# An encoder in fp32 from three products: one more seven-product pair in each first half of down, and two kept differences made in place

## The chip, the cores and the metric

The kernel runs on one core of a Trainium2 chip. The metric is the device time of one execution in microseconds. The names of the engines are those of the profile: PE (TensorE, the matmuls), DVE (VectorE), ACT (ScalarE), POOL (GpSimd) and SP (SyncE, which here only issues transfers).

## The reference

Two encoder layers over 256 tokens of width 2048 in float32. Each has an attention (differential attention in layer 0, windowed grouped-query attention with a sink in layer 1), a cross-attention of four heads into 256 memory tokens, an output projection, and an MLP of width 8192:

```python
for i in range(DEPTH):
    h = rms_norm(x, norm_attn[i])
    mn = rms_norm(mem, norm_mem[i])
    mkv = (mn @ w_mem_kv[i]).reshape(B, MEM_LEN, 2, N_MEM_HEADS, MEM_HEAD_DIM)
    ...
    heads = jnp.concatenate([o.reshape(B, S, MIX_WIDTH), o_m.reshape(B, S, MEM_WIDTH)], axis=-1)
    x = x + heads @ w_out[i]
    h = rms_norm(x, norm_mlp[i])
    x = x + jnp.square(jax.nn.relu(h @ w_up[i])) @ w_down[i]
```

The change touches the last line's second product ("down"), and a little of the key normalisation in layer 1 and of `mn @ w_mem_kv`.

## The kernel before

**The arithmetic.** A float32 value is split into a high part (a cast on ACT, L450) and a low part (the rest, a subtraction on DVE, L451). A product is three matmuls: high by high, low by high, high by low (L542, L543 and L544 in the projections with pairs; L503 to L505 in the others). The two splits of every weight piece of 128x1024 are the main work of ACT and DVE.

**Pairs.** Two pieces of weights and the hidden features that go with them form a 2x2 product of blocks. A plain pair does it with eight products, 24 matmuls of 128x512. A "fast" pair, in `seven`, does it with seven, 21 matmuls; for that it needs sums of weight pieces (`a` and `b`, L364 and L365 on DVE, each then split) and differences of hidden features. Part of the sums is made ahead in DRAM by POOL's transfers (`make_sums`, L299 a copy and L303 an accumulating add; the buffers are called `madesum`).

**Stages.** Each layer goes through the input projection with attention, the output projection, up (eight chunks), and down. Down has two halves of the output (half 0 and half 1), each of 32 pairs j. In the profiled execution layer 0's half 0 is 763 to 927 us and its half 1 927 to 1089; layer 1's are 1738 to 1902 and 1902 to 2062. The tuple `LATE` names the 19 fast pairs of half 1, and `FAST` those of half 0: they follow a pattern of two fast pairs and one plain.

**Differences that are kept.** Half 0 and half 1 need the same differences of hidden features. `keep` makes them (`differences`: L553, L555, L556 and a split) while up still runs, and ACT's queue stores them to DRAM (L1071, `kept<-h`); POOL's queue reads them back two pairs ahead of their use (`load_kept`, L1186, `h<-kept`). A small scheduler runs such steps: `tick` is called between pairs, and a `Task` waits for a number of ticks. For the last chunks of up the waits are in `KEEP_LAST`, so that the differences of j=28 and j=29 are made after the start of down.

**Hidden features that are away.** The features of chunks 6 to 14 go to DRAM too (`hid`), and SP brings them back (L375, `t2k<-hid`) into a ring of eight buffers `t2k`. SP's queue is in order: a load that waits for its buffer holds up all behind it. So are the loads of weights (`raw`, L395; `blk` and `big`, L343) and of `madesum` (L346) on the same queue. An engine's instructions also run in the order written; the order of the program is fixed when it is built.

**Keys and memory.** In layer 1 the keys are normalised by `norm_T`, whose steps wait `ROWS_GAP` between them and end with the transposes of L664 on PE. The memory tokens are loaded by `load_mem` and split by `make_x2` in a part of their own (`mem_part`).

Of the kernel before, what the change touches and what calls it, by code (L numbers as in the profile page):

```python
# [15 lines left out]
F32R = mybir.dt.float32r  # L16
# [6 lines left out]
P = 128  # L23
# [15 lines left out]
WAIT = 2  # L39
# [11 lines left out]
AHEAD = 2  # L51
WARM = 10
LATE = (2, 4, 5, 7, 8, 10, 11, 13, 14, 16, 17, 19, 20, 22, 23, 25, 26, 28, 29)
FAST = tuple(j for j in LATE if j not in (11, 20))
AWAY = range(6, 15)
LATE_BLK = LATE[2::2]
LOOK = 3
MORE = 3
KEEP_AFTER = (2, 6, 10, 14)
KEEP_LAST = (10, 18, 26, 34)  # L60
KEEP_GAP = 2
SUM_AT = {0: 44, 1: 2}
SUM_GAP = ({"in": 4, "mem": 4, "out": 4, "up": 9}, {"in": 4, "mem": 8, "out": 10, "up": 7})
# [11 lines left out]
def trunk(ctx: ExitStack, tc: tile.TileContext, xin, xtok, memin, memtok, posrel, gcol, rows,  # L75
# [104 lines left out]
    def Light(f, gap):  # L180
        return Stage(f, gap, gap, True)
# [271 lines left out]
    def make_x2(X2, k, src, g):  # L453
        t = X2.new(k)
        split_gain(t[:, 0, :], t[:, 1, :], src, g)
# [175 lines left out]
                nc.vector.tensor_tensor(u[n][t], own[n][t], u[n][t], op=ALU.add)  # L631
        return u

    def norm_T(ps, st, nseg, g, later=False):

        dim = 512 // nseg
        qn = []
        hi = blk([P, 4, S], F32R)
        lo = blk([P, 4, S], F32R)

        ms = small(2 * nseg)

        def squares():
            for t in range(2):
                sq = t2k([P, 512])
                nc.scalar.activation(sq, ps[t], AF.Square)
                m = ms[:, t * nseg:(t + 1) * nseg]
                nc.vector.tensor_reduce(m, sq.rearrange("p (n d) -> p n d", d=dim), axis=AX.X, op=ALU.add)
                nc.vector.tensor_scalar(m, m, 1.0 / dim, st[:, t:t + 1], op0=ALU.mult, op1=ALU.add)

        def rows():
            rs = small(2 * nseg)
            inv_sqrt(rs, ms, 2 * nseg)
            for t in range(2):
                q = t2k([P, 512])
                nc.vector.tensor_tensor(q.rearrange("p (n d) -> p n d", d=dim), ps[t].rearrange("p (n d) -> p n d", d=dim),
                                        rs[:, t * nseg:(t + 1) * nseg].unsqueeze(2).broadcast_to([P, nseg, dim]), op=ALU.mult)
                qn.append(q)

        def tr():  # L660
            for t in range(2):
                pt = bank()
                for h in range(4):
                    nc.tensor.transpose(out=pt[:, h * P:(h + 1) * P], in_=qn[t][:, h * P:(h + 1) * P], identity=ident)  # L664
                ts = slice(t * P, (t + 1) * P)
                split_gain(hi[:, :, ts], lo[:, :, ts], pt.rearrange("p (h s) -> p h s", s=P), g)

        if not later:
            squares()
        return (hi, lo), Task([Light(squares, 1), Light(rows, ROWS_GAP), tr][not later:], wait=WAIT if later else 1, gap=WAIT)  # L670

    def val_f32(v, ps, st):
        for t in range(2):
# [293 lines left out]
    def load_mem(i):  # L967
        mem_raw[i] = quad("h2", (P, 4, S), F32)
        nc.sync.dma_start(mem_raw[i], memin[:, 1024 * i:1024 * i + 1024].rearrange("p (k s) -> p k s", s=S))

    def mem_ahead(j):
        if j == 5:
            load_mem(0)

    def mem_part(layer, qm, qd, H2):
        M2 = Halves()

        def before(j):
            if j % 2 == 0:
                if j:  # L980
                    mem_raw.pop(j // 2 - 1)
                if j < 6:
                    load_mem(j // 2 + 1)
            for k in (2 * j, 2 * j + 1):
                src = mem_raw[j // 2][:, k % 4, :]
                make_x2(M2, k, src, gc[:, G_MEM + layer * KT + k:G_MEM + layer * KT + k + 1])

        ps = chunk_tok(f"mem{layer}", 0, M2, before)
        kT, kd = norm_T(ps, mst, 4, gc[:, G_MK + layer:G_MK + layer + 1], layer == 0)
        vbox = [None, None]  # L990
        heads = [plain_head(h, h, qm, kT, vbox, None, None, H2, 12 + h) for h in range(4)]
        firsts = [Task(h[:2], (qd, kd)) for h in heads]
        ps = chunk_tok(f"mem{layer}", 1, M2)
        flush([kd])
        vbox[0], vbox[1] = val_split(ps, mst)
        for i, h in enumerate(heads):
            done_heads[12 + i] = Task(h[2:], [firsts[i]])
# [54 lines left out]
    def mlp(layer, X2, last):  # L1052
# [7 lines left out]
        def hidden(j):  # L1060
            return hT[j // 2].rearrange("p k s -> p (k s)")[:, (j % 2) * 512:(j % 2) * 512 + 512]

        def keep(j, wait):

            def make():
                box.append(quad("h2", (P, 2, 512)))
                differences(box[0], hidden(j))

            def store():
                kept[j] = dp.tile([P, 2, 512], F32R, name=nm("kept"))  # L1070
                nc.scalar.dma_start(as32(kept[j]), as32(box.pop()))  # L1071

            box = []
            Task([Light(make, KEEP_GAP), Light(store, 0)], wait=wait)

        def h2_of(j):
            t2 = quad("h2", (P, 2, 512))
# [11 lines left out]
        def to_hidden(q, n, u, i, tag):  # L1089
            c = 2 * q + n  # L1090
            if i == 0:
                hT.append(wide[:, 5] if c == 15 else blk([P, 4, S], F32))
            pt = bank(tag)
            for oo in range(2):
                for t in range(2):
                    o = 2 * i + oo
                    nc.tensor.transpose(out=pt[:, oo * S + t * P:oo * S + (t + 1) * P], in_=u[n][t][:, o * P:(o + 1) * P], identity=ident)  # L1097
            j = 2 * c + i
            nc.scalar.activation(hidden(j), pt, AF.Relu)
            nc.scalar.activation(hidden(j), hidden(j), AF.Square)  # L1100
            if c in AWAY:
                hidden_in[j] = dp.tile([P, 512], F32, name=nm("hid"))
                nc.gpsimd.dma_start(hidden_in[j], hidden(j))
            if any(j in fast_pairs(f"down{layer}", h) for h in range(2)):
                keep(j, KEEP_AFTER[2 * n + i] if q < 7 else KEEP_LAST[2 * n + i])

        for q in range(8):
            tag, other = ("mm", "aux") if q % 2 == 0 else ("aux", "mm")
# [43 lines left out]
        for half_ in range(2):  # L1152
# [28 lines left out]
            diff_in = {}  # L1181

            def load_kept(j):
                if j in fast:
                    diff_in[j] = quad("h2", (P, 2, 512))
                    nc.gpsimd.dma_start(diff_in[j], kept[j])  # L1186

            load_kept(1)
            for j in range(32):
# [4 lines left out]
                    ats.append(h2_of((j + 1) % 32))  # L1194
                load_kept(j + 2)
                two.append(piece(f"down{layer}", half_, 2 * j + 1))
                at = ats.popleft()
                if last and half_ == 1 and j >= 30:
                    held.append((j, two, at))
# [62 lines left out]
    for g in range(3):  # L1262
# [20 lines left out]
        kT, kd = norm_T(ps, st0, 8, gc[:, G_AK:G_AK + 1])  # L1283
        for h in range(4):
            done_heads[4 * g + h] = Task(diff_head(h, qT, kT, v, bias, H2, 4 * g + h), [qd, kd] + rows_done)
    ps = chunk_tok("a", 9, X2, mem_ahead)
    qm, qd = norm_T(ps, st0, 4, gs[:, 2:3])
    mem_part(0, qm, qd, H2)
    X2 = out_proj(0, H2)
# [6 lines left out]
    make_sums(1)  # L1296
    kv = key_values(X2)
    row_stats(st1)
    kT, kd = norm_T(kv[0], st1, 4, gc[:, G_BK:G_BK + 1])
    vv = val_split(kv[1], st1)  # L1300
    for g in range(3):
        ps = chunk_tok("b", g, X2)
        qT, qd = norm_T(ps, st1, 4, gs[:, 1:2])
        for h in range(4):
            n = 4 * g + h
            done_heads[n] = Task(plain_head(h, n // 3, qT, kT, vv, bias, sink[:, n:n + 1], H2, n), [qd, kd])
    ps = chunk_tok("b", 3, X2, mem_ahead)
    qm, qd = norm_T(ps, st1, 4, gs[:, 3:4])
    mem_part(1, qm, qd, H2)
    X2 = out_proj(1, H2)  # L1310
# [71 lines left out]
```

## Time and profile before

| what | us |
|---|---|
| median of 3 runs | 2066.44 (2066.3 to 2066.57) |
| the profiled execution | 2068.06 |
| its span, first to last instruction | 2066.3 |
| PE busy | 2059.5 (100%) |
| DVE busy | 1824.9 (88%) |
| ACT busy | 1295.9 (63%) |
| POOL busy | 190.5 (9%) |

PE's busy time counts matmuls that overlap, and so a busy share of 100% doesn't say that each takes as long as its row shows. The profile's list of waits says for what an engine stood idle; the windows give each engine's busy time in a stretch; the timeline has single instructions with their start, length, and the idle time before them. The granted clock of PE was 1.000 throughout.

### The profile page before, as it was taken

How to read it: one execution, taken by the hardware profiler on the slowest of the kernel's cores; microseconds unless marked ns; L12 is line 12 of the kernel's file. 1: busy time of each engine (PE TensorE's matmuls, PEld its weight loads, DVE VectorE, ACT ScalarE, POOL GpSimd, SP SyncE). 2: the span in 40 equal slices, each digit the busy share in tenths (PEclk: the TensorE clock that was granted, in tenths of full speed). 3: DMA queues.
4: the chain of work that ended last, by engine and by line, in shares of the span. 5: the costliest groups of instructions: out<-in, count | busy, mean ns of one | idle time of the engine just before them, and what ended most of it. 6: DMA issues, size and time to landing. Idle time of an engine off the chain costs nothing.

```text
span 2066.3 us, 28900 instructions
## 1 busy us (share of the span) xinstructions
PE 2059.5 (100%) x9966; PEld 1711.5 (83%) x9966; DVE 1824.9 (88%) x2659; ACT 1295.9 (63%) x1933; POOL 190.5 (9%) x292
## 2 busy tenths in 40 slices
PE   9999999999999999999999999999999999999999
PEld 7888888888888888888888888888888888888887
DVE  7677787898998999999999778889999999999998
ACT  7467665556566576767756556556566566676764
POOL 1200111100011100000002110000001111000000
PEclk9999999999999999999999999999999999999999
DMA  9678997877898998989978887577799999898994
GB/s 318 242 240 269 279 290 227 276 232 245 277 292 285 308 322 300 389 282 322 365 295 274 262 251 262 174 234 244 246 296 298 311 306 349 309 379 308 329 374 144
DMA packets 176099, 589.08 MB, mean 285 GB/s; under 512 B 20464, under 2 KB 21488, under 8 KB 174576
## 3 DMA queue, kind: packets, MB, share of 16 engines
q1 hardware_dynamic: 134128, 439.36, 59.5%
q0 software_dynamic: 36208, 127.94, 23.7%
q10 hardware_dynamic: 5616, 19.93, 2.4%
q8 instruction: 78, 1.28, 0.2%
q14 instruction: 69, 0.57, 0.1%
HBM read 552.42 MB, written 108.13 MB: 320 GB/s over the span
## 4 chain that ended last, share of the span: by engine, by line
PE 94%; DVE 3%; DMA 2%; issue 1%; ACT 1%; SPq 0%; DVEq 0%; ACTq 0%
PE mm L543 12%; PE mm L544 12%; PE mm L542 12%; PE aux L544 11%; PE aux L542 11%; PE aux L543 11%; PE mm L503 6%; PE mm L504 6%; PE mm L505 6%; DVE lo L451 1%; PE aux L687 1%; PE mm L1097 1%; PE aux L664 1%; PE aux L1097 1%; DMA kept<-h 1%
## 5 line engine op out<-in xcount | busy, mean ns | idle before, releaser
L451 DVE TENSOR_TENSOR lo<-raw,hi 128x1024 fp32r<-128x1024 f32 (+1 forms) x492 | 583.5, 1205 | 116.6 <-ACT hi L450 115.7
L450 ACT CAST hi<-raw 128x1024 fp32r<-128x1024 f32 (+1 forms) x492 | 495.6, 1035 | 287.8 <-PE mm L505 95.7
L503 PE MATMUL mm<-hi,x 128*128 128x512 f32 x576 | 231.5, 404 | 0.1
L504 PE MATMUL mm<-lo,x 128*128 128x512 f32 x576 | 225.6, 392 | 0.2 <-DVE lo L451 0.2
L505 PE MATMUL mm<-hi,x 128*128 128x512 f32 x576 | 225.2, 391 | 0.0
L450 ACT CAST h<-big 128x1024 fp32r<-128x1024 f32 (+1 forms) x100 | 100.4, 1021 | 131.7 <-DVE big L291 84.3
L542 PE MATMUL mm<-hi,x 128*128 128x512 f32 x464 | 181.3, 391 | 0.0
L543 PE MATMUL mm<-lo,x 128*128 128x512 f32 x464 | 180.7, 389 | 0.0
L544 PE MATMUL mm<-hi,x 128*128 128x512 f32 x464 | 180.6, 389 | 0.0
L543 PE MATMUL mm<-lo,h 128*128 128x512 f32 (+1 forms) x448 | 174.2, 389 | 1.3 <-DVE lo L451 1.3
L542 PE MATMUL mm<-hi,h 128*128 128x512 f32 (+1 forms) x448 | 174.1, 389 | 0.0
L544 PE MATMUL mm<-hi,h 128*128 128x512 f32 (+1 forms) x448 | 173.7, 388 | 0.0
L450 ACT CAST hi<-big 128x1024 fp32r<-128x1024 f32 (+1 forms) x138 | 120.8, 902 | 77.1 <-PE aux L544 35.9
L542 PE MATMUL aux<-hi,x 128*128 128x512 f32 x400 | 156.3, 391 | 0.0
L544 PE MATMUL aux<-hi,x 128*128 128x512 f32 x400 | 155.7, 389 | 0.0
L543 PE MATMUL aux<-lo,x 128*128 128x512 f32 x400 | 155.7, 389 | 0.0
L542 PE MATMUL aux<-hi,h 128*128 128x512 f32 x392 | 152.8, 390 | 0.0
L544 PE MATMUL aux<-hi,h 128*128 128x512 f32 x392 | 152.5, 389 | 0.0
L543 PE MATMUL aux<-lo,h 128*128 128x512 f32 x392 | 152.5, 389 | 0.0
L451 DVE TENSOR_TENSOR lo<-big,hi 128x1024 fp32r<-128x1024 f32 (+1 forms) x138 | 139.6, 1032 | 6.8 <-ACT hi L450 6.4
L451 DVE TENSOR_TENSOR h<-big,h 128x1024 fp32r<-128x1024 f32 (+1 forms) x100 | 116.8, 1179 | 30.8 <-ACT h L450 30.0
L505 PEld LDWEIGHTS mm<-hi,x 128*128 128x128 f32 x576 | 108.1, 188 | 23.8 <-DVE x L447 0.2
(318 smaller groups left out, 4452.5 us busy)
## 6 DMA issues: line engine op xcount, KB each, us to landing
raw<-in_w_up SPq DMA_DIRECT2D x164, 512.0 KB, 6.5
madesum<-in_w_down POOLq DMA_DIRECT2D x140, 512.0 KB, 6.6
raw<-in_w_down SPq DMA_DIRECT2D x112, 512.0 KB, 6.5
big<-in_w_up SPq DMA_DIRECT2D x92, 512.0 KB, 5.0
raw<-in_w_a SPq DMA_DIRECT2D x72, 512.0 KB, 5.3
h<-kept POOLq DMA_DIRECT2D x72, 512.0 KB, 6.9
raw<-in_w_out SPq DMA_DIRECT2D x52, 512.0 KB, 5.3
big<-in_w_down SPq DMA_DIRECT2D x46, 512.0 KB, 5.7
```

What stands on the lines that cost most here:

```text
L450: nc.scalar.copy(hi, src)
L451: return nc.vector.tensor_tensor(lo, src, as32(hi), op=ALU.subtract)
L503: nc.tensor.matmul(ps[t], lhsT=xh, rhs=hi[:, ws], start=(k == 0), stop=False)
L504: nc.tensor.matmul(ps[t], lhsT=xh, rhs=lo[:, ws], start=False, stop=False)
L505: nc.tensor.matmul(ps[t], lhsT=xl, rhs=hi[:, ws], start=False, stop=(k == KT - 1))
L542: nc.tensor.matmul(acc_, lhsT=x(0), rhs=w2[0][:, ws], start=first_, stop=False)
L543: nc.tensor.matmul(acc_, lhsT=x(0), rhs=w2[1][:, ws], start=False, stop=False)
L544: nc.tensor.matmul(acc_, lhsT=x(1), rhs=w2[0][:, ws], start=False, stop=last_)
L664: nc.tensor.transpose(out=pt[:, h * P:(h + 1) * P], in_=qn[t][:, h * P:(h + 1) * P], identity=ident)
L687: nc.tensor.transpose(out=pt[:, kt * S + qt * P:kt * S + (qt + 1) * P], in_=p_of(qt)[:, kt * P:(kt + 1) * P], identity=ident)
L1097: nc.tensor.transpose(out=pt[:, oo * S + t * P:oo * S + (t + 1) * P], in_=u[n][t][:, o * P:(o + 1) * P], identity=ident)
```

## The change

1. `FAST` leaves out only pair 26 of `LATE`, where it left out 11 and 20: half 0 of down has 18 fast pairs instead of 17 in each layer, and the kernel 74 instead of 72 in all. Pair 26 becomes plain in half 0, and 11 and 20 become fast.
2. The differences for j=28 and 29 are no longer made at the start of down. In half 0 `make_kept` makes them two pairs ahead of their use, from the hidden features that SP brought back, and uses them from where they are; then they are stored for half 1. Half 0 doesn't read them back.
3. The key normalisation of layer 1 asks for a gap of two steps instead of one ahead of its transposes.
4. The memory tokens are loaded one step sooner, and split one step sooner.

```diff
--- before.py
+++ after.py
-FAST = tuple(j for j in LATE if j not in (11, 20))
+FAST = tuple(j for j in LATE if j != 26)
...
-KEEP_LAST = (10, 18, 26, 34)
+KEEP_LATE = (28, 29)
...
-    def norm_T(ps, st, nseg, g, later=False):
+    def norm_T(ps, st, nseg, g, later=False, rows_gap=ROWS_GAP):
...
-        return (hi, lo), Task([Light(squares, 1), Light(rows, ROWS_GAP), tr][not later:], wait=WAIT if later else 1, gap=WAIT)
+        return (hi, lo), Task([Light(squares, 1), Light(rows, rows_gap), tr][not later:], wait=WAIT if later else 1, gap=WAIT)
...
-    def mem_ahead(j):
-        if j == 5:
-            load_mem(0)
+    mem_x2 = {}
+
+    def memory(layer, j):
+        if j == 0:
+            mem_x2[layer] = Halves()
+        if j % 2 == 0:
+            if j:
+                mem_raw.pop(j // 2 - 1)
+            if j < 6:
+                load_mem(j // 2 + 1)
+        for k in (2 * j, 2 * j + 1):
+            src = mem_raw[j // 2][:, k % 4, :]
+            make_x2(mem_x2[layer], k, src, gc[:, G_MEM + layer * KT + k:G_MEM + layer * KT + k + 1])
+
+    def mem_ahead(layer):
+
+        def ahead(j):
+            if j == 4:
+                load_mem(0)
+            if j == 7:
+                memory(layer, 0)
+
+        return ahead
...
         def before(j):
...
+            if j < 7:
+                memory(layer, j + 1)
...
+        def store_kept(j, t2):
+            kept[j] = dp.tile([P, 2, 512], F32R, name=nm("kept"))
+            nc.scalar.dma_start(as32(kept[j]), as32(t2))
...
-            Task([Light(make, KEEP_GAP), Light(store, 0)], wait=wait)
+            Task([Light(make, KEEP_GAP), Light(lambda: store_kept(j, box.pop()), 0)], wait=wait)
...
             if any(j in fast_pairs(f"down{layer}", h) for h in range(2)):
-                keep(j, KEEP_AFTER[2 * n + i] if q < 7 else KEEP_LAST[2 * n + i])
+                if j not in KEEP_LATE:
+                    keep(j, KEEP_AFTER[2 * n + i])
...
             def load_kept(j):
-                if j in fast:
+                if j in fast and (half_ or j not in KEEP_LATE):
                     diff_in[j] = quad("h2", (P, 2, 512))
                     nc.gpsimd.dma_start(diff_in[j], kept[j])
+
+            def make_kept(j):
+                if half_ == 0 and j in KEEP_LATE:
+                    diff_in[j] = quad("h2", (P, 2, 512))
+                    differences(diff_in[j], hids[j])
+                    Task([Light(lambda t2=diff_in[j]: store_kept(j, t2), 0)], wait=KEEP_GAP)
...
                 two.append(piece(f"down{layer}", half_, 2 * j + 1))
+                make_kept(j + 2)
...
-    ps = chunk_tok("a", 9, X2, mem_ahead)
+    ps = chunk_tok("a", 9, X2, mem_ahead(0))
...
-    kT, kd = norm_T(kv[0], st1, 4, gc[:, G_BK:G_BK + 1])
+    kT, kd = norm_T(kv[0], st1, 4, gc[:, G_BK:G_BK + 1], rows_gap=2)
...
-    ps = chunk_tok("b", 3, X2, mem_ahead)
+    ps = chunk_tok("b", 3, X2, mem_ahead(1))
```

**DVE, start of down's half 0 in layer 0.** The first four rows are pair 10's; then stands the second of the two kept differences, j=29, and behind it the pieces of pair 11. `lo`, `x` and `h` are low parts of weights, of sums and of hidden features; `blk1672` holds the hidden features of j=29. Before:

```order
L451 TENSOR_TENSOR lo1762_8271<-blk1657_7819,hi1761_8270 128x1024 [waits Activation_49]
L451 TENSOR_TENSOR h21768_8288<-blk1240_5908,h21768_8288 128x512 [waits DMASW3_49]
L451 TENSOR_TENSOR x21767_8281<-blk1656_7818,x21766_8280 128x1024 [waits Activation_49]
L451 TENSOR_TENSOR lo1770_8292<-t2k1734_8141,hi1769_8291 128x512 [waits PE_49]
L553 TENSOR_TENSOR t2k1772_8320<-blk1672_7870 128x256
L555 TENSOR_TENSOR t2k1772_8320<-blk1672_7870,t2k1772_8320 128x128 [waits DVE_49]
L556 TENSOR_TENSOR t2k1772_8320<-blk1672_7870,t2k1772_8320 128x128 [waits DVE_49]
L451 TENSOR_TENSOR h21771_8319<-t2k1772_8320,h21771_8319 128x512 [waits Activation_49]
L451 TENSOR_TENSOR lo1775_8328<-raw1773_8326,hi1774_8327 128x1024 [waits DMAHW2_49,Activation_49]
L451 TENSOR_TENSOR h21778_8338<-blk1240_5908,h21778_8338 128x512 [waits DMASW4_49,DMASW2_49,Activation_49]
```

After, from the same row of pair 10:

```order
L451 TENSOR_TENSOR lo1761_8269<-blk1658_7821,hi1760_8268 128x1024 [waits Activation_49]
L451 TENSOR_TENSOR h21767_8286<-blk1240_5908,h21767_8286 128x512 [waits DMASW5_49]
L451 TENSOR_TENSOR x21766_8279<-big980_4688,x21765_8278 128x1024 [waits Activation_49]
L451 TENSOR_TENSOR lo1770_8292<-t2k1733_8137,hi1769_8291 128x512 [waits PE_49]
L364 TENSOR_TENSOR big980_4688<-big980_4688 128x512 [waits DMAHW5_49,DMAHW1_49]
L451 TENSOR_TENSOR x21776_8330<-big980_4688,x21775_8329 128x1024 [waits PE_49,Activation_49]
L365 TENSOR_TENSOR big980_4688<-big980_4688,t2k1744_8188 128x512 [waits DVE_49]
L451 TENSOR_TENSOR h21779_8339<-blk1240_5908,h21779_8339 128x512 [waits DMASW6_49,PE_49]
```

The three rows of the differences, L553, L555 and L556, and the split behind them are gone from this place, and those of j=28, some 25 rows ahead, are gone as well; the sums of pair 11, a fast one now, follow.

**DVE, the end of half 0 in layer 0, after the change.** The first row is the split of the second sum of pair 25 (`x21925`); `t2k1941` holds the hidden features of j=28, `t2k1951` those of j=29, `lo1931` is the low part of the first piece of pair 26:

```order
L451 TENSOR_TENSOR x21925_8980<-big980_4688,x21924_8979 128x1024 [waits Activation_49]
L451 TENSOR_TENSOR lo1928_8991<-t2k1889_8834,hi1927_8990 128x512 [waits PE_49]
L451 TENSOR_TENSOR h21934_9030<-t2k1921_8973,h21934_9030 128x512 [waits DMAHW4_49]
L451 TENSOR_TENSOR h21942_9068<-t2k1933_9026,h21942_9068 128x512 [waits DMAHW7_49,DMASW0_49,Activation_49]
L553 TENSOR_TENSOR t2k1947_9078<-t2k1941_9064 128x256 [waits DMAHW0_49]
L555 TENSOR_TENSOR t2k1947_9078<-t2k1941_9064,t2k1947_9078 128x128 [waits DVE_49]
L556 TENSOR_TENSOR t2k1947_9078<-t2k1941_9064,t2k1947_9078 128x128 [waits DVE_49]
L451 TENSOR_TENSOR h21946_9077<-t2k1947_9078,h21946_9077 128x512 [waits Activation_49]
L553 TENSOR_TENSOR t2k1960_9134<-t2k1951_9112 128x256 [waits DMAHW6_49]
L555 TENSOR_TENSOR t2k1960_9134<-t2k1951_9112,t2k1960_9134 128x128 [waits DVE_49]
L556 TENSOR_TENSOR t2k1960_9134<-t2k1951_9112,t2k1960_9134 128x128 [waits DVE_49]
L451 TENSOR_TENSOR lo1931_9020<-raw1929_9018,hi1930_9019 128x1024 [waits Activation_49]
```

Two sets of differences now stand here, and the second waits for a transfer.

**SP, the same place.** Before, with the hidden features of j=28 and 29 in `t2k1942` and `t2k1950`:

```order
L375 DMA t2k1942_9073<-hid1674_7878 128x512 [waits DMAHW3_49,DMASW0_49,DVE_49]
L395 DMA raw1968_9200<-in_w_down 128x1024 [waits DMAHW4_49,DVE_49]
L395 DMA raw1972_9209<-in_w_down 128x1024 [waits DMAHW5_49,DVE_49]
L375 DMA t2k1950_9111<-hid1676_7887 128x512 [waits DMAHW6_49,DMASW1_49,DVE_49]
L346 DMA big980_4688<-madesum840_4055 128x1024 [waits DMAHW7_49,DVE_49]
L343 DMA big980_4688<-in_w_down 128x1024 [waits DMAHW0_49,DVE_49]
L346 DMA big980_4688<-madesum865_4161 128x1024 [waits DMAHW1_49,DVE_49]
```

After, with those of j=28 and 29 in `t2k1941` and `t2k1951`:

```order
L375 DMA t2k1941_9064<-hid1675_7881 128x512 [waits DMAHW0_49,DMASW2_49,DVE_49]
L343 DMA big980_4688<-in_w_down 128x1024 [waits DMAHW1_49,DVE_49]
L395 DMA raw1938_9060<-in_w_down 128x1024 [waits DMAHW2_49,DVE_49]
L395 DMA raw1943_9071<-in_w_down 128x1024 [waits DMAHW3_49,DVE_49]
L343 DMA blk1659_7822<-in_w_down 128x1024 [waits DMAHW4_49,DVE_49]
L346 DMA big980_4688<-madesum886_4256 128x1024 [waits DMAHW5_49,DVE_49]
L375 DMA t2k1951_9112<-hid1677_7890 128x512 [waits DMAHW6_49,DMASW3_49]
L395 DMA raw1971_9208<-in_w_down 128x1024 [waits DMAHW0_49,DVE_49]
```

The load for j=29 stood ahead of the sum loads (`madesum840`, `madesum865`), and now stands behind three loads more, the last of them `madesum886`.

**PE, the key transposes of layer 1.** Before:

```order
L503 MATMUL mm2440_11300<-hi2451_11333,x22019_9428 128x512 [waits Activation_49]
L504 MATMUL mm2440_11300<-lo2452_11334,x22019_9428 128x512 [waits DVE_49]
L664 MATMUL aux2454_11353<-ident_76,t2k2448_11328 128x128 [waits DVE_49]
L664 MATMUL aux2454_11353<-ident_76,t2k2448_11328 128x128 x3
L505 MATMUL mm2440_11300<-hi2451_11333,x22019_9428 128x512
L664 MATMUL aux2455_11360<-ident_76,t2k2449_11330 128x128 [waits DVE_49]
L664 MATMUL aux2455_11360<-ident_76,t2k2449_11330 128x128 x3
L503 MATMUL mm2441_11301<-hi2451_11333,x22019_9428 128x512
```

After:

```order
L503 MATMUL mm2443_11308<-hi2454_11341,x22022_9436 128x512 [waits Activation_49]
L504 MATMUL mm2443_11308<-lo2455_11342,x22022_9436 128x512 [waits DVE_49]
L664 MATMUL aux2460_11379<-ident_76,t2k2451_11336 128x128 [waits DVE_49]
L664 MATMUL aux2460_11379<-ident_76,t2k2451_11336 128x128 x3
L505 MATMUL mm2443_11308<-hi2454_11341,x22022_9436 128x512
L664 MATMUL aux2461_11386<-ident_76,t2k2452_11338 128x128 [waits DVE_49]
L664 MATMUL aux2461_11386<-ident_76,t2k2452_11338 128x128 x3
L503 MATMUL mm2444_11309<-hi2454_11341,x22022_9436 128x512
```

The rows stand in the same order.

More of the change, by code (lines that the diff above doesn't have):

```diff
@@ L969, in load_mem @@
         nc.sync.dma_start(mem_raw[i], memin[:, 1024 * i:1024 * i + 1024].rearrange("p (k s) -> p k s", s=S))
-    def mem_ahead(j):
-        if j == 5:
-            load_mem(0)
+    mem_x2 = {}
[17 more added lines that the diff above has]
+        return ahead
     def mem_part(layer, qm, qd, H2):
-        M2 = Halves()
+        M2 = mem_x2[layer]
         def before(j):
[L979 to L986, printed above, removed]
+            if j < 7:
+                memory(layer, j + 1)
         ps = chunk_tok(f"mem{layer}", 0, M2, before)
@@ L1067, in make @@
                 differences(box[0], hidden(j))
-            def store():
-                kept[j] = dp.tile([P, 2, 512], F32R, name=nm("kept"))
-                nc.scalar.dma_start(as32(kept[j]), as32(box.pop()))
             box = []
-            Task([Light(make, KEEP_GAP), Light(store, 0)], wait=wait)
+            Task([Light(make, KEEP_GAP), Light(lambda: store_kept(j, box.pop()), 0)], wait=wait)
         def h2_of(j):
```

## The prediction

> **What bounds the kernel now.** I read the page's busy times first, then TensorE's waits, then the windows of the four halves of down, and last the timeline around each wait.
>
> ```profile
> span 2066.3 us, 28900 instructions
> PE 2059.5 (100%) x9966; PEld 1711.5 (83%) x9966; DVE 1824.9 (88%) x2659; ACT 1295.9 (63%) x1933; POOL 190.5 (9%) x292
> ...
> PE 94%; DVE 3%; DMA 2%; issue 1%; ACT 1%; SPq 0%; DVEq 0%; ACTq 0%
> ```
> ```profile
> PE mm L543 <- DVE lo L451: 1.3, 2, 0.8
> PE aux L142 <- DVE ones L139: 1.1, 1, 1.1
> PE aux L664 <- DVE t2k L656: 0.7, 1, 0.7
> PE mm L504 <- DVE lo L451: 0.2, 1, 0.2
> PE aux L687 <- DVE t2k L805: 0.2, 1, 0.2
> ```
> TensorE works from end to end, and its named waits sum to 3.5 us of 2066.3. So an edit can win only in two ways: by taking matmuls away, or by taking these waits away. It can lose as much as it likes, if it puts a new wait on TensorE.
>
> ```profile
> 763.20:927.20 164.00, 163.18 (x728) 134.73 (x727) 155.03 (x186) 111.18 (x142) 9.57 (x18) 1.00 0.92 329
> 927.20:1088.60 161.40, 161.40 (x722) 133.94 (x721) 155.54 (x186) 111.67 (x146) 13.08 (x21) 1.00 0.92 329
> 1738.20:1902.00 163.80, 163.30 (x729) 134.81 (x728) 155.97 (x188) 111.57 (x141) 9.57 (x19) 1.00 0.93 337
> 1902.00:2062.00 160.00, 160.00 (x716) 132.84 (x715) 153.05 (x180) 103.99 (x128) 9.48 (x18) 1.00 0.81 291
> ```
> These are down's halves 0 and 1 of both layers (window, length, then busy time of PE, PEld, DVE, ACT, POOL, the granted clock 1.00, the DMA share). VectorE is the runner-up: in layer 0's half 0 it idles 164.00 − 155.03 = 8.97 us. Half 1 does 19 fast pairs with 155.54 busy of 161.40, and TensorE doesn't wait there at all (161.40 of 161.40).
>
> **1. One more fast pair in each first half: −1.36 us.** A plain pair issues 24 matmuls of 128x512 and a fast one 21, so two layers lose 6. A matmul's own duration is no price, since they overlap; the spacing is:
>
> ```profile
> 1054.28 0.39 PE L543 MATMUL aux<-lo,h 128*128 128x512 f32 x1
> 1054.50 0.39 PE L544 MATMUL aux<-hi,h 128*128 128x512 f32 x1
> 1054.73 0.39 PE L542 MATMUL mm<-hi,h 128*128 128x512 f32 x1
> 1054.96 0.39 PE L543 MATMUL mm<-lo,h 128*128 128x512 f32 x1
> ...
> 1059.49 0.39 PE L542 MATMUL mm<-hi,h 128*128 128x512 f32 x1
> ```
> From 1054.73 to 1059.49 one fast pair passes: 4.76 us for 21, or 0.227 each. Six make 1.36; by the duration of 0.39 they would make 2.3. The Trainium skill's "TensorE: Matmul & The Clock Gate", section "Back-to-back issue gap", gives a sustained spacing of about 131 ns at N=512, and about 216 ns for an isolated one; by the first, six matmuls would be an estimated 0.79 us and the sum 0.57 us less. This trace, with its granted clock of 1.00, shows 227 ns, and I take the trace.
>
> The pair costs VectorE more. Its rows in 850 to 920 are:
>
> ```profile
> L451 DVE TENSOR_TENSOR x<-big,x 128x1024 fp32r<-128x1024 f32 x10 | 12.1, 1214 | 0.0
> L451 DVE TENSOR_TENSOR h<-t2k,h 128x512 fp32r<-128x512 f32 x11 | 7.3, 679 | 0.0
> ```
> ```profile
> 1049.87 1.22 DVE L451 TENSOR_TENSOR x<-big,x 128x1024 fp32r<-128x1024 f32 x1
> 1051.01 0.68 DVE L451 TENSOR_TENSOR lo<-t2k,hi 128x512 fp32r<-128x512 f32 x1
> 1051.61 0.68 DVE L364 TENSOR_TENSOR big<-big 128x512 f32<-128x512 f32 x1
> ```
> Start to start these are 1.14 and 0.60. A plain pair is two splits of 1024 and one hidden split of 512, 2.88; a fast one three of 1024 and four of 512 (two sums, half a piece, the hidden), 5.82. So VectorE gets 2.94 more in each half 0: 155.03 + 2.94 = 157.97 busy in about 162 us. Half 1 shows that 155.54 in 161.40 runs without a wait; 4 us of room against its 5.9 is less, but room it is. I cost it at nothing; its cover is the lead that VectorE has over TensorE, and if that is gone, each missing us is one of TensorE. The GpSimd queue's extra copy and add fall at the end of up, ahead of its first loads there; the additional load of half a megabyte of sums and the kept loads dropped nearly cancel in a half that moves 164 x 329 = 54 MB.
>
> **2. The last two kept differences leave the start of down: −1.86 us.** The waits at TensorE's L543 stand there:
>
> ```profile
> 792.84 0.33 ACTq L1071 DMA_DIRECT2D kept<-h  x1
> ...
> 799.02 0.62 ACT L450 CAST h<-blk 128x512 fp32r<-128x512 f32 x1 [2.79 <-DMA kept<-h]
> ...
> 800.63 1.22 DVE L451 TENSOR_TENSOR x<-big,x 128x1024 fp32r<-128x1024 f32 x1 [1.41 <-ACT x L450]
> ...
> 804.78 0.39 PE L542 MATMUL mm<-hi,h 128*128 128x512 f32 x1
> ...
> 805.99 0.50 PE L543 MATMUL mm<-lo,h 128*128 128x512 f32 x1 [0.82 <-DVE lo L451]
> ```
> ```profile
> 1779.48 0.39 PE L542 MATMUL mm<-hi,h 128*128 128x512 f32 x1
> 1780.37 0.50 PE L543 MATMUL mm<-lo,h 128*128 128x512 f32 x1 [0.50 <-DVE lo L451]
> ```
> The store of a kept difference holds its buffer for 6 us, ScalarE's next hidden cast waits 2.79 for that buffer, VectorE then 1.41 for ScalarE's sum, and TensorE in the end 0.82. Start to start TensorE loses 1.21 − 0.23 = 0.98, and 0.11 more since the released matmul takes 0.50 and not 0.39, together 1.09; in layer 1, 0.66 and 0.11, 0.77. The changed order has neither the store nor the differences there, and VectorE is spared this in the same thin stretch:
>
> ```profile
> 814.54 0.41 DVE L553 TENSOR_TENSOR t2k<-blk 128x256 f32<-128x256 f32 x1
> 814.99 0.29 DVE L555 TENSOR_TENSOR t2k<-blk,t2k 128x128 f32<-128x128 f32 x1
> 815.31 0.29 DVE L556 TENSOR_TENSOR t2k<-blk,t2k 128x128 f32<-128x128 f32 x1
> 816.29 0.69 DVE L451 TENSOR_TENSOR h<-t2k,h 128x512 fp32r<-128x512 f32 x1 [0.69 <-ACT h L450]
> ```
> That is 2.4 us with its wait, twice. It pays for the 2.94 of the fast pair at j=11 before that comes. Bounds: both waits go whole (−1.86), or none goes (0) if another buffer is as late. I take −1.86: the store is the only late step of the chain, and it is 2.79 late against 1.1 lost.
>
> **3. The same differences at j=26 and 27: +1.2 us, and the unknown of this sum.** VectorE now makes the difference for j=29 in line, from hidden features that come from DRAM. In the changed order that load stands on SP behind the second sum load of pair 25, whose buffer VectorE frees with the split `x<-big` of pair 25's second sum. Between that split and the L553 that waits for the load VectorE has seven rows, four splits of 512 and the other difference's three, 3.4 us of work. Before, the same load went out 20 us ahead of its use:
>
> ```profile
> 884.81 0.33 SPq L375 DMA_DIRECT2D t2k<-hid  x1
> ```
> ```profile
> 904.92 0.68 DVE L451 TENSOR_TENSOR h<-t2k,h 128x512 fp32r<-128x512 f32 x1
> ```
>
> The half 1 rows above give the positions in the pattern that half 0 now has at j=25. The split of the second sum ends at 1051.09, 3.64 ahead of pair 25's first matmul (1054.73) and 8.40 ahead of pair 26's (1059.49). The sum load goes out ahead of the hidden one, 0.33 on the queue, so the hidden load issues 8.0 ahead of pair 26. With a landing time L, three difference rows (1.0) and the first split of pair 26 (1.2), that split is ready at L − 5.8 past the start of pair 26, where its second matmul needs it at 0.2. TensorE's new wait is about L − 5.8 where that is positive. Landings of this load, by window (855 to 890, 830 to 860, 985 to 1052):
>
> ```profile
> DMA to landing us min/median/max: 4.2/6.2/8.9
> ...
> DMA to landing us min/median/max: 5.8/6.6/8.7
> ...
> DMA to landing us min/median/max: 4.5/5.6/6.2
> ```
> So 0 at 4.2, 0.4 at 6.2, 0.8 at 6.6, 3.1 at 8.9, in each layer. I take 0.6, between the medians of the two windows of half 0, which have the same DMA share: +1.2. The range is 0 to +6.2. What VectorE loses here it has back in the two plain pairs 26 and 27, which cost it 2.88 each of 5.45. The store on ScalarE's queue stands behind the difference, and hidden casts behind the store; they are a pair ahead of their use, so 0.
>
> **4. Key transposes and memory splits: 0.** The wait at L664 is this one:
>
> ```profile
> 1142.61 0.39 PE L504 MATMUL mm<-lo,x 128*128 128x512 f32 x1
> 1143.67 0.66 PE L664 MATMUL aux<-ident,t2k 128*128 128x128 f32 x4 [0.68 <-DVE t2k L656]
> ```
> It costs 1.06 − 0.22 = 0.84. The diff asks for a gap of 2 instead of 1, but in the order both kernels issue the transposes behind the very same matmuls, and VectorE's rows ahead of them are the same. So 0, with −0.84 as the other end. The memory splits do move in layer 1, but TensorE has no wait in the memory projection; 0, at best the 0.2 of L687.
>
> **The sum.** −1.36 − 1.86 + 1.2 + 0 = −2.0 us. The profiled execution took 2068.06 with its span of 2066.3; it stands 1.62 over the median of the runs, and the difference is carried to the median: 2066.44 − 2.0 = 2064.4.
>
> **The rivals.**
> - *The hidden load lands under its cover.* The 4.2 in the window 855 to 890 and all of 985 to 1052 but its upper end speak for it; the medians of half 0 against it. Then −3.2: 2063.2. The Trainium skill's "DMA: Bandwidth & Descriptors", section "Anatomy of one DMA — SWDGE (gpsimd) path", fits 2.0 us plus bytes/436e3; an estimate by it for these 256 KB is 2.6 us, and it would make this rival certain. That fit is for another queue than SP's, and no landing of this load in the windows above is under 4.2, so it adds little to the chance.
> - *The hidden load lands late and the first half turns into a loss.* It is slower than before when the two new waits exceed 3.2, so from L = 7.4 in each layer. At 8.9 the sum is −3.2 + 6.2, or 2069.4. To pass 0.2% the wait would have to be 3.7 in each layer, a landing of 9.5, which none of these windows shows.
> - *The key transposes do get their rows in time*, through other timing ahead of them: −0.84, and with the first rival 2062.4. The unchanged order speaks against it.
> - *Moving the differences doesn't remove the start's wait*, because another late buffer or a late load takes its place: 2064.4 + 1.86 = 2066.3. VectorE's idle of 1.41 having one releaser speaks against it.
>
> **How the numbers follow.** Forecast 0.45; load under cover 0.25; transposes too 0.08; the start's wait stays 0.10; late load 0.12, of which beyond 0.2% less than half. A change of 0.2%, 4.1 us, is what a measurement of this kernel can tell from none; only the third rival with some more gain comes near 2062.3, and only the worst of the second passes 2070.6: faster 0.07, same 0.88, slower 0.05. The range of 8 in 10 goes from 2062.6 (the first rival less 0.6) to 2068.0 (new waits of 2.4 in each layer).
>
> **What would show it.** TensorE's waits on L543 near 806 and 1780 are gone; the count of matmuls is 6 lower; VectorE's L553 stands near 890 with idle time ahead of it put down to `t2k<-hid`, and TensorE waits for a `lo<-raw` just behind (right if it is under 1.5, wrong if it is absent or over 3); L664 keeps its 0.7. The prediction fails if TensorE shows waits for VectorE through the first 60 us of half 0, or anywhere outside these places.

## The result, and the profile after

The changed kernel takes 2064.28 us (median of 22 runs, 2063.13 to 2065.58), the kernel before 2067.76 (22 runs, 2066.07 to 2071.83): a ratio of 0.9983 with an interval of 0.9977 to 0.9989, or 3.5 us less (2.3 to 4.8). The range held the time. The three runs of before that the prediction started from, 2066.3 to 2066.57, lie at the low end of the 22, and the profiled execution of before, 2068.06, is nearer to their median; so the predicted time was met more closely than the predicted change of 2.0. The two profiled spans, 2066.3 and 2063.0, differ by 3.3.

The first lines of the page, and TensorE's waits, after the change:

```profile
span 2063.0 us, 28957 instructions
...
PE 2056.9 (100%) x9960; PEld 1710.7 (83%) x9960; DVE 1829.8 (89%) x2667; ACT 1299.4 (63%) x1937; POOL 193.6 (9%) x294
```
```profile
PE aux L142 <- DVE ones L139: 1.1, 1, 1.1
PE aux L664 <- DVE t2k L656: 0.6, 1, 0.6
PE mm L503 <- ACT hi L450: 0.6, 1, 0.6
PE mm L504 <- DVE lo L451: 0.2, 1, 0.2
PE aux L687 <- DVE t2k L805: 0.2, 1, 0.2
PE mm L543 <- DVE blk L451: 0.2, 1, 0.2
```
Six matmuls are gone (9966 to 9960), and so are both waits for `lo` at the start of down, 0.8 and 0.5. The key transposes' wait at L664 stands. Two small waits are new, and neither is at a place that the change moved: the one at L503 is in the first 10 us, the one at L543 in the output projection of layer 0.

The windows of half 0 in layers 0 and 1, with the columns of before:

```profile
762.80:926.10 163.30, 163.30 (x730) 135.51 (x729) 159.43 (x193) 116.12 (x147) 9.58 (x18) 1.00 0.94 340
1736.50:1900.20 163.70, 163.70 (x732) 135.69 (x731) 160.19 (x193) 116.43 (x146) 10.11 (x19) 1.00 0.96 344
```
TensorE shows no idle time in them. VectorE is busy 159.43 of 163.30, where 158 of 162 had been worked out.

The unknown of the sum was the difference for j=29, which waits for its hidden features. VectorE there in layer 0, and the issue of the load on SP:

```profile
888.69 0.69 DVE L451 TENSOR_TENSOR h<-t2k,h 128x512 fp32r<-128x512 f32 x1 [0.74 <-ACT h L450]
889.47 0.43 DVE L553 TENSOR_TENSOR t2k<-t2k 128x256 f32<-128x256 f32 x1
...
890.92 4.63 DVE L451 TENSOR_TENSOR lo<-raw,hi 128x1024 fp32r<-128x1024 f32 x4 [0.36 <-ACT hi L450]
```
```profile
885.60 0.38 SPq L375 DMA_DIRECT2D t2k<-hid  x1
```
The landing times of this one load in layer 0 and in layer 1 (the view of the line in a window that holds it alone), then VectorE and TensorE in layer 1:

```profile
DMA to landing us min/median/max: 3.9/3.9/3.9
...
DMA to landing us min/median/max: 4.2/4.2/4.2
```
```profile
1862.82 0.43 DVE L553 TENSOR_TENSOR t2k<-t2k 128x256 f32<-128x256 f32 x1 [0.40 <-DMA t2k<-hid]
...
1863.96 4.63 DVE L451 TENSOR_TENSOR lo<-raw,hi 128x1024 fp32r<-128x1024 f32 x4
```
```profile
1867.06 0.39 PE L542 MATMUL mm<-hi,h 128*128 128x512 f32 x1
...
1867.97 0.39 PE L543 MATMUL mm<-lo,h 128*128 128x512 f32 x1
```
The row of TensorE in layer 0 that takes the same split as the last one above:

```profile
895.29 0.39 PE L543 MATMUL mm<-lo,h 128*128 128x512 f32 x1
```
The load landed after 3.9 and 4.2 us, and VectorE waited 0.40 in layer 1 and not at all in layer 0. The tightest of the splits behind it is the second one: it starts 1.14 after 1863.96 and ends 1.22 later, at 1866.32, and TensorE takes it at 1867.97, 1.65 later. So TensorE would wait from a landing of 4.2 + 1.65 = 5.85 us on in layer 1. In layer 0 the same split ends at 890.92 + 1.14 + 1.22 = 893.28, TensorE takes it at 895.29, and VectorE had waited 0.36 for ScalarE ahead of it: the limit there is 3.9 + 2.01 + 0.36, about 6.3. The prediction had worked out 5.8. That is near, but luck has a part in it. It dropped the 0.2 that it names itself: by its own positions TensorE waits from 6.0 on. It took the first split, which in layer 1 has 0.46 more room than the second. And its load went out 8.0 us ahead of pair 26, where 8.8 and 8.4 were measured. Its landing time was further off.

### The profile page after: what moved, and what is told of

Its sections match the earlier page's. It is cut to its first block, busy times and chain, and to the rows that moved or that the text cites. A ratio compares the mean times of both kernels' runs of the same rounds, so it can differ in the third digit from the quotient of the medians.

```text
span 2063.0 us, 28957 instructions
## 1 busy us (share of the span) xinstructions
PE 2056.9 (100%) x9960; PEld 1710.7 (83%) x9960; DVE 1829.8 (89%) x2667; ACT 1299.4 (63%) x1937; POOL 193.6 (9%) x294
## 4 chain that ended last, share of the span: by engine, by line
PE 93%; DVE 3%; DMA 2%; issue 1%; ACT 1%; SPq 0%; DVEq 0%; ACTq 0%
PE mm L543 12%; PE mm L544 12%; PE mm L542 12%; PE aux L543 11%; PE aux L542 11%; PE aux L544 11%; PE mm L503 6%; PE mm L504 6%; PE mm L505 6%; DVE lo L451 1%; DMA raw<-in_w_kv 1%; PE aux L1111 1%; PE mm L1111 1%; PE aux L687 1%; PE aux L664 1%
## 5 line engine op out<-in xcount | busy, mean ns | idle before, releaser
L503 PE MATMUL mm<-hi,x 128*128 128x512 f32 x576 | 231.4, 404 | 0.6 <-ACT hi L450 0.6
L543 PE MATMUL mm<-lo,x 128*128 128x512 f32 x464 | 180.7, 389 | 0.0
L542 PE MATMUL mm<-hi,h 128*128 128x512 f32 (+1 forms) x436 | 169.5, 389 | 0.0
L543 PE MATMUL mm<-lo,h 128*128 128x512 f32 (+1 forms) x436 | 169.2, 388 | 0.0
L544 PE MATMUL mm<-hi,h 128*128 128x512 f32 (+1 forms) x436 | 169.1, 388 | 0.0
L543 PE MATMUL aux<-lo,x 128*128 128x512 f32 x400 | 155.8, 389 | 0.0
L543 PE MATMUL aux<-lo,h 128*128 128x512 f32 x394 | 153.4, 389 | 0.0
```

What stands on the lines that cost most here:

```text
L503: nc.tensor.matmul(ps[t], lhsT=xh, rhs=hi[:, ws], start=(k == 0), stop=False)
L542: nc.tensor.matmul(acc_, lhsT=x(0), rhs=w2[0][:, ws], start=first_, stop=False)
L543: nc.tensor.matmul(acc_, lhsT=x(0), rhs=w2[1][:, ws], start=False, stop=False)
L544: nc.tensor.matmul(acc_, lhsT=x(1), rhs=w2[0][:, ws], start=False, stop=last_)
```

## The experiments

**One part of the change alone.** First the kernel before with the new `FAST` and nothing else:

```diff
-FAST = tuple(j for j in LATE if j not in (11, 20))
+FAST = tuple(j for j in LATE if j != 26)
```


> The kernel before with FAST of the changed kernel alone; the kept differences of j=28 and 29 stay at the start of down. Theory A (VectorE has no slack in the first 70 us of half 0, and only the moved differences make room for the fast pair at j=11): the six matmuls give -1.4 us, but TensorE waits for VectorE on L543 between 805 and 850 us and again in layer 1, 1 to 3 us in each layer beyond the 0.82 and 0.50 of before: -1.4 + 2 to 6, so between +0.6 and +4.6 us against the kernel before. Rival B (the two parts simply add): -1.4 us, and the L543 waits stay near 0.8 and 0.5.

It took 2081.25 us against 2068.47 of before (ratio 1.0066, 1.0053 to 1.0079): 13 to 14 us more, far beyond either expectation. TensorE's waits for VectorE in down:

```profile
PE mm L543 <- DVE lo L451: 9.5, 13, 1.1
...
PE aux L544 <- DVE h L451: 0.8, 2, 0.4
...
PE aux L543 <- DVE lo L451: 0.5, 1, 0.5
```
They stand between 790 and 874 us and between 1772 and 1855; the rest of each half 0 has none. VectorE is what TensorE waits for, and yet it idles 12.5 us in half 0 of layer 0 (busy 157.46 of 763.2 to 933.2). Its longest idle time there, and ScalarE's just ahead of it:

```profile
831.52 0.62 ACT L450 CAST h<-t2k 128x512 fp32r<-128x512 f32 x1 [3.79 <-DMA t2k<-hid]
```
```profile
833.12 1.23 DVE L451 TENSOR_TENSOR x<-big,x 128x1024 fp32r<-128x1024 f32 x1 [2.62 <-ACT x L450]
```
So theory A holds in its cause, but its price was much too low. VectorE doesn't only get 2.94 us more work: it stands behind ScalarE, which stands behind a load of hidden features. Earlier in the half the store of the kept difference is in the chain as before: a hidden cast waits 3.57 for it, VectorE 2.18 and TensorE 1.00, at 807.76. A late VectorE frees its buffers late, and what is loaded into them then comes late too; that this closes the loop is argued from the rows, and no run took it apart.

Then the kernel before with the moved differences (`KEEP_LATE`, `make_kept`) and nothing else.

> The kernel before with the moved differences alone; FAST, the key gap and the memory splits as before. Theory A: the two waits at the start of down go, -1.9 us against the kernel before, and no new wait comes at the end of half 0. Rival B: pair 26 is fast here, VectorE has no two plain pairs to make the differences in, and TensorE waits 0.5 to 2 us in each layer near 895 and 1868 us: -0.9 to +2.1 us.

It took 2065.92 against 2068.47 (0.9989, 0.9980 to 0.9998), 2.5 us less with an interval of 0.4 to 4.1. Its whole list of waits:

```profile
PE aux L142 <- DVE ones L139: 1.1, 1, 1.1
PE aux L664 <- DVE t2k L656: 0.7, 1, 0.7
PE mm L504 <- DVE lo L451: 0.2, 1, 0.2
PE aux L687 <- DVE t2k L805: 0.2, 1, 0.2
PE mm L505 <- DVE x L447: 0.2, 1, 0.2
```
Both waits at L543 are gone and no new one stands at the end of half 0: theory A. Rival B's wait doesn't come, but its case did not come up either. Here pair 26 is fast, and the build put VectorE's two differences 10 us apart; the one for j=29 stands far behind its load, which went out at 888.27 and landed after 3.8 us:

```profile
890.70 0.42 DVE L553 TENSOR_TENSOR t2k<-t2k 128x256 f32<-128x256 f32 x1
...
900.73 0.41 DVE L553 TENSOR_TENSOR t2k<-t2k 128x256 f32<-128x256 f32 x1
```
```profile
DMA to landing us min/median/max: 3.8/3.8/3.8
```
In the changed kernel, with pair 26 plain, the two stand 2.6 us apart (886.88 and 889.47), right behind the load. So the tight place belongs to the two parts together.

Both of these parts, without the key gap and the memory's changes:

> The changed kernel with the key gap of 1 and the memory loads and splits as before. Theory A (these two parts are worth nothing, as TensorE doesn't wait in the memory projection and the transposes stand at the same place): the same time as the changed kernel within 0.5 us, some 3.5 below the kernel before, with L664 waiting 0.6 to 0.7. Rival B: they carry a part of the gain, and this kernel is 0.8 us or more slower than the changed one.

It took 2064.83 against 2068.47 (0.9983, 0.9974 to 0.9992), the ratio of the changed kernel. On top of start_only the fast pairs give 2065.92 − 2064.83 = 1.1 us by the medians of 11 runs each, near the 1.36 of six matmuls; the ranges overlap (2064.62 to 2067.04, and 2063.76 to 2065.33), so the size is rough. With the start of down freed, the same `FAST` that cost 13 us alone now gains. One wait in this profile spoke against my zero for the memory splits:

```profile
PE mm L503 <- ACT x L446: 1.7, 1, 1.7
```
It is in the memory projection, between 1200 and 1320 us. L664's wait, which was expected at 0.6 to 0.7, is absent from this profile, though the transposes stand where they stood.

**The cause of the waits at the start.** The kernel before, with the differences of j=28 and 29 made and not stored; both halves read those of j=26 in their place:

```diff
             def store():
+                if j in (28, 29):
+                    box.pop()
+                    kept[j] = kept[26]
+                    return
                 kept[j] = dp.tile([P, 2, 512], F32R, name=nm("kept"))
```


> The kernel before, with the differences of j=28 and 29 still made at the start of down but not stored: both halves read those of j=26 in their place, so those two pairs compute with the wrong differences. Theory A (the wait at TensorE comes from the store, which holds its buffer for 6 us and so ScalarE's next cast): the two waits on L543 go, and the time falls by 1.9 us or so against the kernel before, as with start_only. Rival B (it comes from VectorE's 2.4 us of work for each difference): the waits stay at 0.5 or more in each layer.

It took 2065.89 against 2067.75 (0.9990, 0.9981 to 0.9999), 1.9 us less with an interval of 0.2 to 3.9. In half 0 of both layers TensorE waits for nothing; the one group for L543 in its list,

```profile
PE mm L543 <- DVE lo L451: 0.4, 2, 0.3
```
is in up, at 1569. VectorE's work for the differences is still there, at the same place in its order, so the store was the cause, not that work. The edit moves one thing more: ScalarE's cast that had waited for the store's buffer, at 799.02 before, now stands two rows sooner in its order, at 793.6, the buffer being free.

**The load for j=29.** The changed kernel, with a second load of the same features behind the first:

```diff
+    once = []
...
             nc.sync.dma_start(hids[k], hidden_in[k])
+            if k == 29 and once:
+                once.pop()
+                nc.sync.dma_start(hids[k], hidden_in[k])
...
+        once[:] = [1]
```


> The changed kernel, with the hidden features of j=29 loaded twice in a row into the same buffer in half 0, the second load waiting for the first, so that VectorE gets them at about 8 to 9 us after the first issue and not at 3.9 and 4.2. Theory A (TensorE's wait is that time less 5.85, by the changed kernel's margin of 1.65 at a landing of 4.2): waits on L543 of 2 to 3 us at about 895 and 1868, and 4 to 6 us in all against the changed kernel, so at or a little above the kernel before. Rival B (the two plain pairs 26 and 27 and the lead hide it): VectorE idles some 4 us, TensorE under 0.5, time of the changed kernel.

It took 2065.11 (ratio 0.9983, 0.9975 to 0.9992, as the changed kernel), and TensorE waited for nothing there. But it isn't rival B's case. VectorE at the place (the lines stand 5 further down, L558 is the differences' first row):

```profile
888.37 0.69 DVE L456 TENSOR_TENSOR h<-t2k,h 128x512 fp32r<-128x512 f32 x1 [0.74 <-ACT h L455]
890.61 4.63 DVE L456 TENSOR_TENSOR lo<-raw,hi 128x1024 fp32r<-128x1024 f32 x4 [1.55 <-ACT hi L455]
...
898.10 0.41 DVE L558 TENSOR_TENSOR t2k<-t2k 128x256 f32<-128x256 f32 x1
```
The build put the second difference behind the four splits of pairs 26 and 27, at 898.10, so nothing stood behind the late load: the edit changed the order, not only the load. The next two keep every engine's order and make the load of j=29 slower, in both halves, by laying its features out in DRAM in small pieces (c = 16, then 8 floats; lines from there on stand 1 to 3 further down, so L546 is L543 and L556 is L553):

```diff
+            if k == 29:
+                nc.sync.dma_start(hids[k].rearrange("p (b c) -> p b c", c=16), hidden_in[k].rearrange("b p c -> p b c"))
+                return
...
+                if j == 29:
+                    hidden_in[j] = dp.tile([512 // 16, P, 16], F32, name=nm("hid"))
+                    nc.gpsimd.dma_start(hidden_in[j].rearrange("b p c -> p b c"), hidden(j).rearrange("p (b c) -> p b c", c=16))
...
```


> The changed kernel with the hidden features of j=29 laid out in DRAM so that their load moves in pieces of 64 bytes, which makes this one load slower in both halves; every engine's order stays as it is. Theory A (TensorE's wait is the landing time less 5.85): at a landing of 9 us a wait of about 3 in each layer, on L543 `lo<-raw` near 895 and 1867 us, and the kernel slower than after_again by the sum of the two; at 7 us about 1 in each. Rival B (the lead and the plain pairs hide it): TensorE's wait stays under a third of that.

Pieces of 64 bytes landed at 5.4 us in layer 0, and at 5.7 in layer 1:

```profile
DMA to landing us min/median/max: 5.4/5.4/5.4
...
DMA to landing us min/median/max: 5.7/5.7/5.7
```
```profile
891.35 0.42 DVE L556 TENSOR_TENSOR t2k<-t2k 128x256 f32<-128x256 f32 x1 [1.69 <-DMA t2k<-hid]
```
VectorE waits 1.69 and 1.97, TensorE not at all, and the time is 2064.70 (0.9983, 0.9974 to 0.9992). That is what limits of 5.85 and 6.3 ask for, but it doesn't tell the theories apart.

> As hid29_slow, in pieces of 32 bytes instead of 64, which landed at 5.4 and 5.7 us with no wait of TensorE. Theory A (wait = landing less 5.85): at a landing of 8 us about 2.1 in each layer, on L543 `lo<-raw` near 895 and 1867 us, and the time 3 to 5 us above the changed kernel; at 7 us 1.1 in each. Rival B (the two plain pairs hide it): under 0.5 in each layer.

Pieces of 32 bytes landed at 8.8 in both layers. VectorE and TensorE in layer 0:

```profile
894.80 0.43 DVE L556 TENSOR_TENSOR t2k<-t2k 128x256 f32<-128x256 f32 x1 [5.08 <-DMA t2k<-hid]
...
895.79 4.62 DVE L454 TENSOR_TENSOR lo<-raw,hi 128x1024 fp32r<-128x1024 f32 x4
```
```profile
894.37 0.39 PE L545 MATMUL mm<-hi,h 128*128 128x512 f32 x1
897.07 0.50 PE L546 MATMUL mm<-lo,h 128*128 128x512 f32 x1 [2.31 <-DVE lo L454]
...
897.63 0.40 PE L545 MATMUL mm<-hi,h 128*128 128x512 f32 x1
898.20 0.50 PE L546 MATMUL mm<-lo,h 128*128 128x512 f32 x1 [0.17 <-DVE lo L454]
```
Start to start, less 0.23 for the matmul, TensorE loses 2.47 and 0.34, and 0.11 at each released matmul: 3.0 in layer 0. Layer 1 loses 2.4 in the same way. The two limits from the changed kernel ask for 8.8 − 6.3 = 2.5 in layer 0 and 8.8 − 5.85 = 2.95 in layer 1: the sum of 5.4 is met, the layers are not, each by half a us. The time from the load's issue to TensorE's row differs from run to run: 9.7 and 9.3 us in the changed kernel's two layers, 9.4 and 9.9 here. The kernel takes 2071.20 against 2069.11 of before (1.0008, 0.9999 to 1.0017): the whole gain is gone, and by the medians about 2 us more. So theory A's limit is shown from both sides, to about half a us, and the plain pairs hide nothing of what is over it.

**The base again, and the key gap.**

> The changed kernel once more, as the base of this group: some 3.5 us below the kernel before, no wait on L543 in down, L664 waiting 0.6 to 0.7.

It took 2064.08 against 2067.75 (0.9983, 0.9974 to 0.9991); L664's wait is 0.4 in this profile. One small wait in down was not expected: TensorE loses 0.28 us at 789.80. The slowest of the kernels above, with pieces of 32 bytes, has one of 0.43 at the same place; the changed kernel's first profile and the others with its order have none there.

```diff
-    kT, kd = norm_T(kv[0], st1, 4, gc[:, G_BK:G_BK + 1], rows_gap=2)
+    kT, kd = norm_T(kv[0], st1, 4, gc[:, G_BK:G_BK + 1], rows_gap=3)
```


> The changed kernel with the key gap of 3 instead of 2. Here the built order does move: the key transposes stand some ten matmuls later. Theory A (a gap of 2 leaves them where they were, and the wait is only that they come 0.6 us too soon): L664's wait goes, and the kernel is 0.6 to 0.9 us faster than after_again. Rival B: what the transposes feed is late next, and TensorE waits as long at another line by 1200 us: no change.

The built order moves here, and the wait at L664 is gone from the list; nothing took its place:

```profile
PE aux L142 <- DVE ones L139: 1.1, 1, 1.1
PE mm L503 <- ACT hi L450: 0.5, 1, 0.5
PE aux L687 <- DVE t2k L805: 0.2, 1, 0.2
```
The median is 2063.25, 0.8 below after_again; the intervals of the two ratios overlap (0.9967 to 0.9986 here), so the profile shows the wait gone, and the times only agree with it. The wait varies by itself: of the ten profiles with a gap of 1 or 2, nine have it, at 0.2 to 0.7; of the four with a gap of 3, none has it.

> The key gap of 3 and the memory loads and splits as before, all else as changed: against key_gap_3 it tells what the sooner memory splits are worth. Theory A (nothing, but pairs_and_start showed one wait of 1.7 us on `x` of L446 at a memory split, and start_only one of 0.3, which the changed kernel's profiles don't have): 0 to 0.5 us slower in the median, with a wait on L446 or L447 between 1200 and 1290 us in the profile. Rival B: 1 us or more slower.

It took 2063.59 in a group whose before is 2069.11 (0.9968, 0.9956 to 0.9981), and its profile has no wait in the memory projection. The sooner memory splits are worth nothing that these medians show. A wait appeared there in two of the six profiles without them, 1.7 and 0.2, and in none of the eight with them; whether they guard against it is open.

**One more fast pair.** The changed kernel with the key gap of 3 and `FAST = LATE`:

> The changed kernel with the key gap of 3 and pair 26 fast as well in half 0, so all 19 of LATE. Theory A (with the start of down freed, VectorE has room for one more: 158 + 2.9 of 162 us): six matmuls fewer, -1.4 us against key_gap_3, the best of all. Rival B (pairs_only showed what happens when VectorE's lead is gone; without two plain pairs the differences at the end of half 0 take it): TensorE waits on L543 after 880 us and in layer 1, 1 to 8 us in all, slower than key_gap_3.

It took 2063.38 against 2069.11 (0.9971, 0.9960 to 0.9983), no faster by its median than key_gap_3, which ran in another group, but not for want of VectorE:

```profile
PE mm L542 <- DMA h<-kept: 1.3, 1, 1.3
```
```profile
1735.83 1.04 POOL L303 DMA_DIRECT2D madesum<-in_w_down  x1 [11.09 <-DMA t2k<-in_w_down]
1736.49 1.52 POOL L1201 DMA_DIRECT2D h<-kept  x2
...
1745.08 0.54 POOL L1201 DMA_DIRECT2D h<-kept  x1 [2.96 <-PE mm L544]
```
No wait for VectorE stands in down. VectorE's two differences stand 10 us apart here too, and 3.2 in key_gap_3 (in layer 0), which differs only in pair 26. The six matmuls are paid back by one wait of layer 1. L1201 is the load of the kept differences, L1186 in the kernel before. The last accumulating add of sums was issued only at 1735.83, and the kept differences' loads, which stand behind it in GpSimd's order, at 1736.49, as half 0 began. The prediction had costed that queue at nothing for one pair more in a layer, and the changed kernel shows no wait for it; for two it costs 1.3. The last run makes the sums sooner:

```diff
-SUM_GAP = ({"in": 4, "mem": 4, "out": 4, "up": 9}, {"in": 4, "mem": 8, "out": 10, "up": 7})
+SUM_GAP = ({"in": 4, "mem": 4, "out": 4, "up": 8}, {"in": 4, "mem": 8, "out": 10, "up": 6})
```


> all_fast_gap_3 with SUM_GAP in up of 8 instead of 9 in layer 0 and 6 instead of 7 in layer 1, so that GpSimd's last copy and add of sums come ahead of the first kept loads. Theory A (the wait of 1.3 us on `h<-kept` at 1745.75 comes from the last sum, which holds up the kept loads behind it on GpSimd's queue): that wait goes, and the kernel is about 1.4 us faster than all_fast_gap_3. Rival B: sums made faster in up take transfers from the loads there, and TensorE waits in up instead: the same or slower.

```profile
PE aux L142 <- DVE ones L139: 1.1, 1, 1.1
PE aux L687 <- DVE t2k L805: 0.2, 1, 0.2
```
It took 2061.65 against 2068.52 (0.9968, 0.9955 to 0.9980): the lowest median of all, with a span (2059.6) 3.4 below that of the changed kernel's profiled run, and two waits are left. GpSimd's adds are gone from the end of up: from 1700 us to the start of down its queue carries hidden features and kept loads alone. Against all_fast_gap_3 (0.9971) the intervals overlap; the profile shows that wait gone, and the times only agree.

## Why the prediction was right or wrong

- **Six matmuls, −1.36: right.** 1.1 by the medians of start_only and pairs_and_start, whose ranges overlap; the count is 6 lower. That the fast pair costs VectorE nothing holds only together with step 2: alone it costs 13 us. The prediction named the cover, the lead of VectorE, but priced its loss at one us of TensorE for each missing us, at most 2.94 in a layer; measured, it is (12.8 + 1.36) / 2, about 7 in each.
- **The start of down, −1.86: right in cause and nearly in size.** no_store gave 1.9 (0.2 to 3.9) and start_only 2.5 (0.4 to 4.1).
- **The differences for j=29, +1.2: the step that failed.** TensorE's wait behind the difference is absent, which the prediction had named as the sign that it is wrong here. The mechanism and its limit stand (5.8 worked out; 5.85 and 6.3 by the changed kernel's rows; 5.4 lost in the two layers at a landing of 8.8), but the landing time of 6.4 was mis-sized: it was 3.9 and 4.2, and the cost 0. In the seven other runs with the moved differences that left this load as it is and issue it once, it was 3.6 to 4.7. The first rival, with 2063.2, was the one that came. I had taken medians of the same load in half 0 of before, and not asked what the change does to the traffic around it. The views of transfers from 885 to 892 us, of before and then of after:

```profile
DMA packets 828, 2.71 MB, mean 387 GB/s; under 512 B 92, under 2 KB 92, under 8 KB 827
...
DMA packets 493, 1.51 MB, mean 215 GB/s; under 512 B 61, under 2 KB 61, under 8 KB 493
```
In that stretch the hidden load took 7.4 us with 2.71 MB moving, and 3.9 with 1.51. The reason isn't that pair 26, now plain, asks for no sums: in start_only and all_fast_gap_3 it is fast, and the load landed after 3.8 us too. While the load was under way, 228 and 217 GB/s moved in these two, 217 in the changed kernel, and 385 in before (all in layer 0). What the three share, against before, is that the load stands two or three loads later in SP's order, and that half 0 no longer reads back the kept differences of j=28 and 29. That the traffic sets the landing time is read from these stretches; no run put the traffic back, and which of the two thinned it is open.
- **Key transposes, 0: right.** The gap of 2 left them at the same place, and the wait stayed; a gap of 3 moves them and takes it away in all four profiles that have it.
- **Memory splits, 0: not contradicted by the medians,** with the open point above.
- **The sum.** −1.36 − 1.86 + 0 + 0 = −3.2, where the spans differ by 3.3 and the medians by 3.5. The forecast of 2064.4 was so close to 2064.28 by luck: the base of 2066.44 was 1.3 too low and the hidden load's term 1.2 too high.

## What to carry to other kernels

A part that loses 13 us alone can gain 1.1 beside another that gives it room: price parts of a change in the order in which they make room for each other, and take a runner-up engine's lead as a stock; here 2.94 us of extra work in a layer, put where the stock was thin, cost TensorE about 7. A wait on a transfer is priced by its limit, which positions in the trace gave to about half a us, and by its landing time, which must be read with the traffic that will be there, not with that of before. And where a scheduler builds the order, look at the built order first: a gap raised by one moved nothing, an edit meant to slow one load moved the work behind it, and whether two differences stand beside each other or 10 us apart hung on one pair being plain or fast.

## What the runs showed of the hardware

At the same place in the kernel, the same 256 KB load took 3.9 to 4.2 us in rows of 2 KB, 5.4 to 5.7 in pieces of 64 bytes, and 8.8 in pieces of 32. In rows of 2 KB it took 7.4 us with 385 GB/s moving while it was under way, and 3.9 with 217. The kernel before varied far more from run to run (2066.07 to 2071.83) than the changed one (2063.13 to 2065.58); the kernels without the store at the start of down stay within 2.7 us, except the one with pieces of 32 bytes, with 4.5; why is open.
